# Moving the four blocks of a small second product from the first two column tiles to the seventh, in a fused decoder layer on one Trainium2 core

## Chip, core and metric

The kernel runs on one core of one Trainium2 chip. A core has TensorE (PE: products, and with a separate row the weight loads PEld), VectorE (DVE), ScalarE (ACT), GpSimd (POOL) and SyncE (SP); the last two here issue DMAs for the most part. The metric is the device time of one execution in microseconds, lower is better; the time of before is the median of three runs.

## The reference

One layer, 512 tokens, width 2048. Cut to what matters:

```python
h = rms_norm(x, norm_gain)
z = h @ w_in                                   # 2048 x 6656
q, k, v, g_attn, c_b, c_c, c_h, g_conv = split(z)
q, k = partial_rope(rms_norm(q)), partial_rope(rms_norm(k))   # heads of 64
y_attn = sliding_window_attention(q, k, v, sinks) * silu(g_attn)   # 16 heads, 4 KV heads, window 128
y_conv = c_b * short_conv(c_c * c_h, conv_w) * silu(g_conv)
x = x + concat([y_attn, y_conv]) @ w_out
gate = sigmoid(rms_norm(x, gate_gain) @ w_ple_gate + b)
e = rms_norm(p @ w_ple_proj, ple_norm_gain)    # p: 512 x 256, w_ple_proj: 256 x 2048
out = x + gate * e
```

`e` is needed only by the last two of the kernel's groups; attention's output is needed by its sixth.

## The kernel before

Everything is fp32, as products of split halves (`wh`, `wl`: ScalarE casts the high half, line 199, VectorE subtracts for the low one, line 200), three matmuls for each product. The kernel has three stages. The first computes K and V and one group of Q's columns. The last computes eight groups by a scheme with seven products in place of eight (line 241). Between them lies the stage that is changed: lines 711 to 905, about 126 to 274 us of the profiled execution.

In this stage a loop computes the first half of c_c and c_h, in column tiles of 128 columns by 512 tokens: `gemm_tile` runs 16 steps `k` of three matmuls each (48 in all, PSUM tile `psg`), and the tiles alternate c_c and c_h. Seven tiles are computed in the loop; the eighth is computed after it (line 1391, PSUM `pst`). Each tile has two weight loads ("jobs") of 512 KB, `raw`. `next_job` splits one job ahead and fetches two more.

After every second `k`, thus every six matmuls, `tick()` advances a clock and runs what was registered for it with `at(when, ...)`, in order of time and then of registration. TensorE's order is just the order in which the Python code emits it; the order on the other four engines in this stage is decided by a scheduler. Registered are:

- `make_k(t)`, ticks 4 and 7: transposes K into PSUM `psm` (one buffer), which ScalarE evicts into `kr` (line 740); then four casts `khh` and four differences `kll`.
- `square_q`, `rstd_q`, `rope_q`: head norm and rotation of the half of Q that is used last.
- `attention(j, n, when)`, 16 units (KV head j, block n), each of four pieces. `scores` (line 794, PSUM `pss`, room for one unit; then VectorE's four reductions, line 800, into `prob`, of which there are two; then ScalarE's exponentials, line 807); `turn` (transposes of `prob` into `pst`, line 822, and halves `pth`, `ptl`); `values` (line 832, PSUM `pso`, copied to `up` and stored by a DMA); and an accumulating DMA. For even n, `turn_q` four ticks earlier transposes Q into the same `psm` and copies it to two tiles `st` (lines 776, 777).
- `e_block(n)`, through a table `mids` that names the tile and the `k` ahead of which it is emitted: 24 matmuls into four PSUM banks (both tiles of `pss`, and two of `pst`). Each bank is then squared with a row sum by ScalarE (line 865), multiplied by the gain `pg` by VectorE (line 867) and stored to memory by a DMA on POOL's queue (line 868).

`up`, `kr`, `yconv`, `pg` and e's tiles share one pool of eleven buffers. At the end of the stage its memory goes to the weight tiles of the last stage (`wy`, `ws`), whose loads wait until the DMAs that read the old tiles have landed.

Of the kernel before, what the change touches and what calls it, by code (L numbers as in the profile page):

```python
# [27 lines left out]
TQ, TK, TV, TGA, TCB, TCC, TCH, TGC = 0, 8, 10, 12, 20, 28, 36, 44  # L28
# [7 lines left out]
def hymba_layer(ctx: ExitStack, tc: tile.TileContext, io):  # L36
# [87 lines left out]
    for g in range(NG):  # L124
        w, n = groups[g]
# [72 lines left out]
    def halves(h, l, src):  # L198
        nc.scalar.copy(h, src)  # L199
        tt(l, src, f32(h), op=ALU.subtract)  # L200
# [259 lines left out]
    def flat(t):  # L460
        return t.rearrange("p a b -> p (a b)")
# [32 lines left out]
    for c in range(8):  # L494
# [20 lines left out]
        for i in range(2):  # L515
            k = 2 * c + i
# [47 lines left out]
    def head_sums(z, out, junk):  # L564

        sq = junk.rearrange("p (h d) -> p h d", d=HD)
        nc.scalar.activation(sq, z, AF.Square)
        nc.vector.tensor_reduce(out, sq, axis=mybir.AxisListType.X, op=ALU.add)

    def head_rstd(ms, eps):  # L570


        stt(ms, ms, 1.0 / HD, eps.unsqueeze(2).broadcast_to(ms.shape), op0=ALU.mult, op1=ALU.add)
        power(ms, ms)
# [8 lines left out]
    def q_of(t, n):  # L583
        return qs[t, n].rearrange("p b (h d) -> p b h d", d=HD)
# [3 lines left out]
    def square_q(t, n, b, junk):  # L588
        if b == 0:
            rq[t, n] = small.tile([P, 2, 8], F32, name="msq", bufs=4)  # L590
        head_sums(q_of(t, n)[:, b], rq[t, n][:, b], junk("sqq"))

    def rstd_q(t, n):
        blocks = slice(2 * t, 2 * t + 2)
        head_rstd(rq[t, n], eps_tok[:, blocks])

    def rope_q(t, n):
        rope(q_of(t, n), 0, slice(2 * t, 2 * t + 2), mtile)
# [5 lines left out]
    for j, s in enumerate((6, 6, 7, 7, 9, 9, 10, 10)):  # L604
        soon(after, s, form7, j)

    jobs = [io["w_in"][TCC, 0], io["w_ple_proj"][0], io["w_in"][TCC, 1], io["w_ple_proj"][1],
            io["w_in"][TCH, 0], io["w_ple_proj"][2], io["w_ple_proj"][3], io["w_in"][TCH, 1]]
    for i in range(1, 4):
        jobs += [io["w_in"][t + i, c] for t in (TCC, TCH) for c in range(2)]  # L610
    raws, splits, job = {}, {}, [0]

    def blocks_of(t):
# [68 lines left out]
    def mtile(name):  # L682
        return misc.tile([P, T], F32, tag="m", name=name)
# [5 lines left out]
    def at(when, fn):  # L689
        later.append((when, len(later), fn))  # L690
# [31 lines left out]
    for t in range(2):  # L722
        rope_q(t, 1)
        for b in range(2):
            at(18 + 2 * t + b, lambda t=t, b=b: square_q(t, 0, b, mtile))
        at(20 + 2 * t, lambda t=t: rstd_q(t, 0))
        at(24 + 2 * t, lambda t=t: rope_q(t, 0))
    mask = cw.tile([P, 2 * P], F32, name="mask", bufs=1)
    nc.gpsimd.dma_start(mask, io["mask"])
    vv = vvp.tile([P, NB, NKV, 2, HD], F32R, name="vv")  # L730
# [51 lines left out]
    def attention(j, n, when):  # L782

        lo = 0 if n else P
        cell = {}

        def scores():
            sc = [ps_s.tile([P, 2, 2 * P], F32, name="pss") for _ in range(2)]
            ks = slice(n * P + lo - P, (n + 1) * P)
            for r in range(4):  # L790
                i = 2 * (n % 2) + r // 2
                q = turned[j, n // 2, r % 2][:, i * P : (i + 1) * P]
                out = sc[r // 2][:, r % 2, lo:]
                nc.tensor.matmul(out, q, khh[j][:, ks], start=True, stop=False)
                nc.tensor.matmul(out, q, kll[j][:, ks], start=False, stop=True)
            t = ap.tile([P, 4, 2 * P], F32, name="prob")
            negm, sums, sk = (small.tile([P, 4], F32, name=x) for x in ("negm", "sums", "sk"))
            r_q = rq[n // 2, j // 2][:, n % 2, 4 * (j % 2) : 4 * (j % 2) + 4]
            for r in range(4):
                nc.vector.tensor_tensor_reduce(  # L800
                    t[:, r, lo:], sc[r // 2][:, r % 2, lo:], mask[:, lo:], HD**-0.5, NEG,
                    ALU.add, ALU.max, negm[:, r : r + 1],
                )
            tt(negm, negm, r_q, op=ALU.mult)
            stt(negm, negm, -1.0, nsink[:, 4 * j : 4 * j + 4], op0=ALU.mult, op1=ALU.min)
            for r in range(4):
                nc.scalar.activation(  # L807
                    t[:, r, lo:], t[:, r, lo:], AF.Exp, scale=r_q[:, r : r + 1], bias=negm[:, r : r + 1],
                    accum_out=sums[:, r : r + 1],
                )  # L810
            tt(sk, sink[:, 4 * j : 4 * j + 4], negm, op=ALU.add)
            nc.scalar.activation(sk, sk, AF.Exp)
            tt(sums, sums, sk, op=ALU.add)
            nc.vector.reciprocal(rs[:, n, 4 * j : 4 * j + 4], sums)
            cell["t"] = t

        def turn():
            cell["pt"] = []
            for kt in range(lo // P, 2):
                pt_ = ps_t.tile([P, T], F32, name="pst")  # L820
                for r in range(4):
                    nc.tensor.transpose(pt_[:, r * P : (r + 1) * P], cell["t"][:, r, kt * P : (kt + 1) * P], ident)  # L822
                h, l = (ap.tile([P, T], F32R, name=x) for x in ("pth", "ptl"))
                halves(h, l, pt_)
                cell["pt"].append((n - 1 + kt, h, l))

        def values():
            po = ps_o.tile([P, 4, P], F32, name="pso")
            pts = cell["pt"]
            for i, (b, h, l) in enumerate(pts):  # L830
                w = vv[:, b, j].rearrange("p s d -> p (s d)")
                nc.tensor.matmul(po, w, h, start=i == 0, stop=False)  # L832
                nc.tensor.matmul(po, w, l, start=False, stop=i == len(pts) - 1)
            up = mtile("up").rearrange("p (r t) -> p r t", t=P)
            nc.scalar.copy(up, po)
            rows = attn_dram[j].rearrange("(r d) (n t) -> d r n t", d=HD, n=NB)[:, :, n]
            nc.gpsimd.dma_start(rows, up[:HD])
            cell["add"] = lambda: nc.gpsimd.dma_start(rows, up[HD:], accum_op=ALU.add)

        if n % 2 == 0:  # L840
            at(when - 4, lambda: turn_q(j, n // 2))
        at(when, scores)
        at(when + 5, turn)
        at(when + 8, values)
        at(when + 12, lambda: cell["add"]())

# [3 lines left out]
    def load_pg(n):  # L850
        pgs.append(mtile("pg"))
        nc.sync.dma_start(pgs[n], io["ple_norm_gain"][:, n * T : (n + 1) * T])

    def e_block(n):

        pg = pgs[n]
        if n < 3:
            load_pg(n + 1)
        ws = next_job()
        banks = [flat(ps_s.tile([P, 2, 2 * P], F32, name="pss")) for _ in range(2)]  # L860
        banks += [ps_t.tile([P, T], F32, name="pst") for _ in range(2)]

        def take_e(t):
            e = mtile("e")
            nc.scalar.activation(e, banks[t], AF.Square, accum_out=esq[:, t, n : n + 1])
            e = mtile("e")
            tt(e, banks[t], pg, op=ALU.mult)
            nc.gpsimd.dma_start(e_dram[t // 2][n][:, t % 2], e)

        for t in range(NB):  # L870
            for k in range(2):
                h, l = (a[:, k, t * P : (t + 1) * P] for a in pts)
                for i, (a, w) in enumerate(((h, ws[0]), (l, ws[0]), (h, ws[1]))):
                    nc.tensor.matmul(banks[t], a, w[:, k], start=k == 0 and i == 0, stop=k == 1 and i == 2)  # L874
            for i in (t,):
                take_e(i)
# [1 line left out]
    load_pg(0)  # L878
    order = [(j, n) for j in (2, 3, 0, 1) for n in range(NB)]
    for u, (j, n) in enumerate(order):  # L880
        attention(j, n, 13 + 35 * u // 15)
    mids = {0: {8: lambda: e_block(0)}, 1: {k: lambda n=n: e_block(n) for n, k in ((1, 0), (2, 4), (3, 8))}}


    for i in range(4):
        ps = gemm_tile(ps_g.tile([P, T], F32, name="psg"), mids.get(2 * i))
        zc = mtile("zc") if i < 3 else rowp.tile([P, T], F32, tag="rows", name="zc")
        tt(zc, ps, rx2, op=ALU.mult)
        if i == 3:
            break  # L890
        ps = gemm_tile(ps_g.tile([P, T], F32, name="psg"), mids.get(2 * i + 1))
        u = cw.tile([P, T + HD], F32, name="u")
        nc.gpsimd.memset(u[:, 0:2], 0.0)
        tt(u[:, 2 : T + 2], ps, zc, op=ALU.mult)
        y = mtile("yconv")
        nc.scalar.activation(y, u[:, 0:T], AF.Copy, scale=convw[:, 0, i : i + 1])
        for s in (1, 2):
            stt(y, u[:, s : s + T], convw[:, s, i : i + 1], y, op0=ALU.mult, op1=ALU.add)
        nc.gpsimd.dma_start(conv_dram[i], y)
# [493 lines left out]
    u, y = itile("u"), rowp.tile([P, T], F32, tag="rows", name="yconv")  # L1393
# [121 lines left out]
```

## Time and profile before

| | |
|---|---|
| median of three runs | 919.99 us (919.91 to 920.25) |
| profiled execution | 919.36 us |
| its span, first to last instruction | 917.6 us |
| granted TensorE clock | 0.998 |
| TensorE busy | 905.9 us, 99% of the span |
| VectorE, ScalarE, GpSimd busy | 723.8, 542.7, 160.8 us |
| DMA | 195.06 MB, mean 213 GB/s |
| this stage begins, and its eighth tile begins | 126.34 us, 274.28 us |

Times in the profile are counted from the span's start. A busy TensorE is modelled from pipelined matmuls: starts are what counts, not durations. A row of the wait list reads: who waited, for whom, microseconds in total, how often, the longest.

### The profile page before, as it was taken

The numbers are of one execution on the slowest core, as the hardware profiler recorded it, in microseconds if no ns is written. First come the engines' busy times: TensorE is split into PE (matmuls) and PEld (weight loads), VectorE is DVE, ScalarE is ACT, GpSimd is POOL, SyncE is SP. The second block draws the span as 40 slices with busy tenths as digits, with TensorE's granted clock in tenths as the row PEclk, the third lists the DMA queues.
The fourth block names the chain that finished last, engine by engine and source line by source line (L and its number), as shares of the span: only waits on it lengthen the run. The fifth ranks groups of instructions, "written<-read, shape, count | busy, mean of one in ns | idle before, by whom it ended". The sixth has DMA issues, their size and how long they took to land.

```text
span 917.6 us, 12067 instructions
## 1 busy us (share of the span) xinstructions
PE 905.9 (99%) x4178; PEld 751.4 (82%) x4178; DVE 723.8 (79%) x1063; ACT 542.7 (59%) x878; POOL 160.8 (18%) x211
## 2 busy tenths in 40 slices
PE   9999999999999999999999999999999999999997
PEld 8888888878888888888888888888888888887885
DVE  6878888788765777877768678987858887889678
ACT  6767847778863443454345357766556666555453
POOL 4232132143230001100120110102120111001100
PEclk9999999999999999999999999999999999999999
DMA  9999558434469767558578887858996993588647
GB/s 315 362 292 308 197 63 309 162 81 108 93 116 313 269 204 234 159 169 233 157 185 240 239 222 233 253 141 229 341 291 193 211 295 92 139 248 267 183 138 218
DMA packets 71389, 195.06 MB, mean 213 GB/s; under 512 B 8355, under 2 KB 14819, under 8 KB 71328
## 3 DMA queue, kind: packets, MB, share of 16 engines
q1 hardware_dynamic: 48096, 132.14, 42.3%
q0 software_dynamic: 23088, 62.15, 30.5%
q8 instruction: 32, 0.52, 0.2%
q14 instruction: 29, 0.24, 0.1%
q10 hardware_dynamic: 144, 0.01, 0.0%
HBM read 162.81 MB, written 31.46 MB: 212 GB/s over the span
## 4 chain that ended last, share of the span: by engine, by line
PE 89%; DVE 6%; ACT 3%; issue 2%; DVEq 0%; ACTq 0%
PE psp L241 67%; PE psg L711 6%; PE psp L519 5%; PE pst L241 4%; PE pst L993 2%; ACT prob L807 1%; PE pss L874 1%; PE pst L1391 1%; PE pst L874 1%; PE pst L822 1%; DVE wl L200 1%; DVE z L1289 1%; DVE prob L800 1%; DVE ptl L200 1%; PE pso L832 1%
## 5 line engine op out<-in xcount | busy, mean ns | idle before, releaser
L241 PE MATMUL psp<-wh,form 128*128 128x512 f32 x1280 | 395.3, 390 | 0.0
L241 PEld LDWEIGHTS psp<-wh,form 128*128 128x128 f32 x1280 | 239.4, 188 | 49.2
L241 PE MATMUL psp<-wl,form 128*128 128x512 f32 x640 | 249.5, 390 | 1.3 <-DVE wl L200 1.2
L200 DVE TENSOR_TENSOR wl<-wy,wh 128x1024 fp32r<-128x1024 f32 x108 | 131.5, 1222 | 60.3 <-ACT wh L199 59.7
L199 ACT CAST wh<-wy 128x1024 fp32r<-128x1024 f32 x108 | 113.4, 1051 | 90.2 <-PE psp L241 70.6
L241 PEld LDWEIGHTS psp<-wl,form 128*128 128x128 f32 x640 | 120.1, 188 | 27.4 <-DVE wl L200 2.5
L200 DVE TENSOR_TENSOR wl<-wx,wh 128x1024 fp32r<-128x1024 f32 x72 | 88.0, 1223 | 50.0 <-ACT wh L199 49.8
L199 ACT CAST wh<-ws 128x1024 fp32r<-128x1024 f32 x72 | 75.9, 1054 | 74.5 <-PE psp L241 53.8
L199 ACT CAST wh<-wx 128x1024 fp32r<-128x1024 f32 x72 | 75.6, 1052 | 74.3 <-PE psp L241 52.7
L241 PE MATMUL psp<-wh,hsh 128*128 128x512 f32 x304 | 118.6, 390 | 0.0
L241 PE MATMUL psp<-wl,hsh 128*128 128x512 f32 x304 | 118.3, 389 | 0.0
L241 PE MATMUL psp<-wh,hsl 128*128 128x512 f32 x304 | 118.3, 389 | 0.0
L200 DVE TENSOR_TENSOR wl<-ws,wh 128x1024 fp32r<-128x1024 f32 x72 | 88.1, 1223 | 27.1 <-ACT wh L199 26.8
L189 DVE TENSOR_TENSOR wy<-wy,ws 128x1024 f32<-128x1024 f32 x72 | 87.7, 1218 | 0.0
L241 PEld LDWEIGHTS psp<-wh,hsh 128*128 128x128 f32 x304 | 57.1, 188 | 11.8
L241 PEld LDWEIGHTS psp<-wh,hsl 128*128 128x128 f32 x304 | 57.1, 188 | 11.8
L241 PEld LDWEIGHTS psp<-wl,hsh 128*128 128x128 f32 x304 | 57.1, 188 | 11.8
L711 PE MATMUL psg<-hsh,wh 128*128 128x512 f32 x112 | 45.2, 403 | 0.0
L711 PE MATMUL psg<-hsh,wl 128*128 128x512 f32 x112 | 43.8, 391 | 0.0
L711 PE MATMUL psg<-hsl,wh 128*128 128x512 f32 x112 | 43.8, 391 | 0.0
L199 ACT CAST wh<-raw 128x1024 fp32r<-128x1024 f32 (+1 forms) x29 | 29.2, 1006 | 22.5 <-DMA raw<-in_w_ple_proj 7.7
L200 DVE TENSOR_TENSOR wl<-raw,wh 128x1024 fp32r<-128x1024 f32 (+1 forms) x29 | 33.8, 1165 | 9.5 <-ACT wh L199 9.2
(218 smaller groups left out, 1307.1 us busy)
## 6 DMA issues: line engine op xcount, KB each, us to landing
ws<-in_w_mid SPq DMA_DIRECT2D x40, 512.0 KB, 4.5
wx<-in_w_mid SPq DMA_DIRECT2D x24, 512.0 KB, 4.2
wy<-in_w_mid SPq DMA_DIRECT2D x20, 512.0 KB, 7.6
h<-form POOLq DMA_DIRECT2D x32, 256.0 KB, 5.8
wy<-in_w_mid POOLq DMA_DIRECT2D x16, 512.0 KB, 8.1
raw<-in_w_in SPq DMA_DIRECT2D x16, 512.0 KB, 4.1
wx<-in_w_out SPq DMA_DIRECT2D x16, 512.0 KB, 7.6
ws<-in_w_out SPq DMA_DIRECT2D x16, 512.0 KB, 5.6
```

The lines of the kernel that those rows point to most:

```text
L189: tt(y, y, got[g, "s1" if f == 6 else "s0", c], op=ALU.add)
L199: nc.scalar.copy(h, src)
L200: tt(l, src, f32(h), op=ALU.subtract)
L241: nc.tensor.matmul(ps[t], a, w[:, i], start=start and first and i == 0 and n == 0, stop=last and i == 1 and n == 2, skip_group_check=not s ...
L519: nc.tensor.matmul(kv_ps[t // 2][:, t % 2], hs[k][a][:, t * P : (t + 1) * P], kv_split[c][w][:, i], start=k == 0 and n == 0, stop=k == KT ...
L711: nc.tensor.matmul(ps, w[:, k % 8], a, start=k == 0 and n == 0, stop=k == KT - 1 and n == 2)
L800: nc.vector.tensor_tensor_reduce(t[:, r, lo:], sc[r // 2][:, r % 2, lo:], mask[:, lo:], HD**-0.5, NEG, ALU.add, ALU.max, negm[:, r : r + 1],)
L807: nc.scalar.activation(t[:, r, lo:], t[:, r, lo:], AF.Exp, scale=r_q[:, r : r + 1], bias=negm[:, r : r + 1], accum_out=sums[:, r : r + 1],)
L822: nc.tensor.transpose(pt_[:, r * P : (r + 1) * P], cell["t"][:, r, kt * P : (kt + 1) * P], ident)
L832: nc.tensor.matmul(po, w, h, start=i == 0, stop=False)
L874: nc.tensor.matmul(banks[t], a, w[:, k], start=k == 0 and i == 0, stop=k == 1 and i == 2)
L993: nc.tensor.transpose(pt[:, b], quads[b // 2][:, b % 2, f * P : (f + 1) * P], ident)
```

## The change

Five edits in one stage, no change of what is computed.

- `mids`: e's blocks 0 to 2 move from tiles 0 and 1 to tile 6, ahead of its steps 8, 10 and 12; block 3 follows after that tile.
- `jobs`: the four loads of `w_ple_proj` stand accordingly at places 13, 15, 16 and 17 of 20 instead of 1, 3, 5 and 6.
- attention's units are registered two ticks earlier (first scores at tick 11 instead of 13); Q's turns, the values and the accumulating DMA move along with them, by two.
- `turn` comes six ticks after its unit's scores instead of five, thus in all one tick earlier than before.
- squares, norm and rotation of Q's other half come three ticks earlier.

```diff
-    jobs = [io["w_in"][TCC, 0], io["w_ple_proj"][0], io["w_in"][TCC, 1], io["w_ple_proj"][1],
-            io["w_in"][TCH, 0], io["w_ple_proj"][2], io["w_ple_proj"][3], io["w_in"][TCH, 1]]
-    for i in range(1, 4):
-        jobs += [io["w_in"][t + i, c] for t in (TCC, TCH) for c in range(2)]
+    jobs = [io["w_in"][t + i, c] for i in range(4) for t in (TCC, TCH) for c in range(2)]
+    jobs[13:14] = [io["w_ple_proj"][0], jobs[13]] + [io["w_ple_proj"][i] for i in range(1, 4)]
...
-            at(18 + 2 * t + b, lambda t=t, b=b: square_q(t, 0, b, mtile))
-        at(20 + 2 * t, lambda t=t: rstd_q(t, 0))
-        at(24 + 2 * t, lambda t=t: rope_q(t, 0))
+            at(15 + 2 * t + b, lambda t=t, b=b: square_q(t, 0, b, mtile))
+        at(17 + 2 * t, lambda t=t: rstd_q(t, 0))
+        at(21 + 2 * t, lambda t=t: rope_q(t, 0))
...
-        at(when + 5, turn)
+        at(when + 6, turn)
         at(when + 8, values)
...
-        attention(j, n, 13 + 35 * u // 15)
-    mids = {0: {8: lambda: e_block(0)}, 1: {k: lambda n=n: e_block(n) for n, k in ((1, 0), (2, 4), (3, 8))}}
+        attention(j, n, 11 + 35 * u // 15)
+    mids = {6: {k: lambda n=n: e_block(n) for n, k in ((0, 8), (1, 10), (2, 12))}}
...
         if i == 3:
+            e_block(3)
             break
```

Below is what stands in a row on the engines at three places. A row is the line, the operation, the tiles written and read, and the size; line numbers after the change are smaller by two.

TensorE around K's second transposes (`psm<-ident,kv`), before and then after the change; `psm<-ident,z` are Q's transposes.

```order
L711 MATMUL psg<-hsl,wh 128x512
L711 MATMUL psg<-hsh,wl 128x512
L739 MATMUL psm<-ident,kv 128x128 x4
L711 MATMUL psg<-hsh,wh 128x512
L711 MATMUL psg<-hsl,wh 128x512
```

```order
L709 MATMUL psg<-hsl,wh 128x512
L709 MATMUL psg<-hsh,wl 128x512
L737 MATMUL psm<-ident,kv 128x128 x4
L770 MATMUL psm<-ident,z 128x128 x4
L709 MATMUL psg<-hsh,wh 128x512
```

Both sets of transposes now follow each other into the one buffer `psm`; and 18 products of c_c stand between the first transposes of K and these, where there were 18 products and an e block.

ScalarE at the same place, before and then after: `wh<-raw` is a weight cast, `kr` evicts `psm`.

```order
L199 CAST wh<-raw 128x1024
L740 ACTIVATE kr<-psm,kq 128x512
L745 CAST khh<-kr 64x512
L746 CAST khh<-kr 64x512
L745 CAST khh<-kr 64x512
L746 CAST khh<-kr 64x512
L865 ACTIVATE e,esq<-pss 128x512 x2
L865 ACTIVATE e,esq<-pst 128x512
L199 CAST wh<-raw 128x1024
L865 ACTIVATE e,esq<-pst 128x512
L740 ACTIVATE kr<-psm,kq 128x512
```

```order
L199 CAST wh<-raw 128x1024
L738 ACTIVATE kr<-psm,kq 128x512
L743 CAST khh<-kr 64x512
L744 CAST khh<-kr 64x512
L743 CAST khh<-kr 64x512
L744 CAST khh<-kr 64x512
L738 ACTIVATE kr<-psm,kq 128x512
L743 CAST khh<-kr 64x512
```

The first eviction keeps its place behind the weight cast; e's four squares and a cast have gone from between the two evictions.

TensorE in attention, at the fourth unit's scores (`pss_2005` before, `pss_1756` after), with buffer numbers; `prob_1863` is the second unit's `prob`, `prob_1572` the first's.

```order
L711 MATMUL psg_1895<-hsl_373,wh_1792 128x512
L711 MATMUL psg_1895<-hsh_372,wl_1793 128x512
L822 MATMUL pst_1987<-ident_208,prob_1863 128x128 x4
L822 MATMUL pst_1996<-ident_208,prob_1863 128x128 x4
L794 MATMUL pss_2005<-khh_1455,st_1835 128x256
```

```order
L820 MATMUL pst_1738<-ident_208,prob_1572 128x128 x4
L709 MATMUL psg_1719<-hsh_252,wh_1609 128x512
L709 MATMUL psg_1719<-hsl_253,wh_1609 128x512
L709 MATMUL psg_1719<-hsh_252,wl_1610 128x512
L709 MATMUL psg_1719<-hsh_258,wh_1609 128x512
L709 MATMUL psg_1719<-hsl_259,wh_1609 128x512
L709 MATMUL psg_1719<-hsh_258,wl_1610 128x512
L792 MATMUL pss_1756<-khh_1455,st_1595 128x256
```

Before, the second unit is already turned when the fourth unit's scores come; after, only the first is, and the second follows the scores.

## The prediction

> **What bounds the kernel now.** I read the page first: engines and chain.
>
> ```profile
> span 917.6 us, 12067 instructions
> PE 905.9 (99%) x4178; PEld 751.4 (82%) x4178; DVE 723.8 (79%) x1063; ACT 542.7 (59%) x878; POOL 160.8 (18%) x211
> PE 89%; DVE 6%; ACT 3%; issue 2%; DVEq 0%; ACTq 0%
> ```
>
> TensorE carries 89% of the chain, so a microsecond counts only if TensorE waits for it. Next the windows over the stage that is changed (about 126 to 274 us), with the columns stretch, length, busy time of PE, PEld, DVE, ACT, POOL, granted clock, DMA share, GB/s.
>
> ```profile
> 126.00:134.00 8.00, 8.00 (x39) 6.63 (x38) 7.08 (x24) 1.98 (x2) 0.00 (x0) 1.00 0.53 26
> 134.00:166.00 32.00, 32.00 (x147) 26.49 (x146) 24.58 (x33) 22.96 (x49) 7.63 (x14) 1.00 0.88 303
> 166.00:246.00 80.00, 77.06 (x445) 65.49 (x444) 65.81 (x238) 65.05 (x176) 24.84 (x27) 1.00 0.43 101
> 246.00:286.00 40.00, 39.81 (x197) 33.16 (x197) 20.40 (x55) 21.77 (x49) 11.92 (x15) 1.00 0.67 159
> ```
>
> In attention's stretch (166 to 246) VectorE and ScalarE are each busy 82% (65.8 and 65.1 of 80) and TensorE loses 2.9 us. In the stretch of e's blocks (134 to 166) TensorE loses nothing. Third, TensorE's waits in this stage (total, times, longest) and the chain in order of time.
>
> ```profile
> PE pst L822 <- DVE ptl L200: 2.4, 3, 1.5
> PE pst L822 <- DVE negm L804: 0.6, 1, 0.6
> PE pso L832 <- ACT up L835: 0.2, 1, 0.2
> ```
>
> ```profile
> 126.34 5.45 PE psg L711 x24
> 131.78 0.44 PE psm L739 x4
> 132.22 2.75 PE pss L874 x12
> 134.98 2.72 PE pst L874 x12
> 137.70 4.08 PE psg L711 x18
> 141.78 0.44 PE psm L739 x4
> ...
> 274.28 10.88 PE pst L1391 x48
> ```
>
> One e block is 2.75 + 2.72 = 5.47 us of products, a tick (six products) 1.36. The stage lasts 274.28 - 126.34 = 147.9 us. Before, 5.5 us of e stand between the first transposes of K (131.78) and the next (141.78).
>
> **The change, part by part.** Four e blocks leave the front and return at the end: 4 x 5.47 us of TensorE work moves, none goes. What matters is what they covered.
>
> *The front.* K's second transposes (make_k(0)) stay at tick 7, but without the block TensorE gets there at 126.34 + 5.45 + 0.44 + 4.08 = 136.3 instead of 141.78. Attention's first turn of Q moves from tick 9 to the same tick 7, directly behind. All three use the single PSUM buffer psm, which is free only when ScalarE has evicted it (L740, kr). ScalarE's rows there:
>
> ```profile
> 135.80 1.05 ACT L199 CAST wh<-raw 128x1024 fp32r<-128x1024 f32 x1 [7.67 <-DMA raw<-in_w_ple_proj]
> 136.75 0.68 ACT L740 ACTIVATE kr<-psm,kq 128x512 f32<-128x512 f32 x1
> ...
> 139.40 0.62 ACT L746 CAST khh<-kr 64x512 fp32r<-64x512 f32 x1
> ```
>
> ScalarE stood 7.67 us for a weight load, and the first kr is queued behind that cast. In the new order the same cast (now of a w_in tile, the fourth load, of the same size, behind the same instructions) stands ahead of kr, so kr again ends at 136.75 + 0.68 = 137.4. TensorE waits 137.5 - 136.3 = 1.2 us. The transposes take 0.44. The new order has the second kr behind four casts khh, the last of which ends at 139.40 + 0.62 = 140.0; kr ends at 140.7, and Q's transposes start then: 140.75 - 137.95 = 2.8 us more. Together 4.0 us. Bounds: 0 if the load landed 4 us sooner; 7.67 is all that ScalarE stood, so up to 7 if it came that much later. I take 4.0, since everything ahead of the load is unchanged.
>
> *The first scores*, now at tick 11, 24 products later: 141.2 + 5.45 = 146.65. They need Q's two halves st, behind the second kr (140.7), four khh, st, one weight cast and two more ScalarE casts, then VectorE's weight difference and st itself. With 0.62, 0.59, 1.05, 1.23 and 0.69 from the rows here and below that ends at 147.2: 0.5 us (bounds 0 to 1.5). Before, e's blocks covered this chain for 22 us.
>
> *The loop.* A unit's scores fill pss (room for one unit); VectorE's four reductions (L800) empty it into prob (two buffers), ScalarE exponentiates, TensorE turns prob into pst, halves follow, then values. The reduction of unit u writes prob's buffer of unit u-2, so it waits for the turn of u-2.
>
> ```profile
> L800 DVE CUSTOM_DVE_ANT_0 prob<-pss,mask 128x256 f32<-128x256 f32 x48 | 17.9, 420 | 2.6 <-PE pst L822 2.4 <-PE pss L795 0.2
> ```
>
> Before, VectorE idled 2.4 us on that. Before, units whose scores are 5 ticks apart from those of u-2 find the turn done; now the turn comes at 6, after scores of u in every unit and exactly one tick ahead of scores u+1 (the spacing is 7 ticks per three units). So the ring is: turn of u-2, reduction of u on VectorE, scores of u+1 on TensorE, with six products (1.36 us) of cover where there were two ticks. Rows of a unit:
>
> ```profile
> 219.69 1.03 PE L822 MATMUL pst<-ident,prob 128*128 128x128 f32 x8
> 223.64 0.42 DVE L800 CUSTOM_DVE_ANT_0 prob<-pss,mask 128x256 f32<-128x256 f32 x1
> 223.99 0.42 DVE L800 CUSTOM_DVE_ANT_0 prob<-pss,mask 128x256 f32<-128x256 f32 x1
> 224.53 1.29 DVE L200 TENSOR_TENSOR ptl<-pst,pth 128x512 fp32r<-128x512 f32 x2
> 226.09 0.59 ACT L807 ACTIVATE prob<-prob,negm,msq 128x256 f32<-128x256 f32 x1
> 226.22 1.23 DVE L200 TENSOR_TENSOR wl<-raw,wh 128x1024 fp32r<-128x1024 f32 x1
> 217.59 0.59 ACT L776 CAST st<-psm 64x512 fp32r<-64x512 f32 x1
> 219.74 0.69 DVE L777 TENSOR_TENSOR st<-psm,st 64x512 fp32r<-64x512 f32 x1
> ```
>
> Reductions start 0.35 us apart: two free half of pss after 0.8 us, four take 1.4 to 1.5. A free VectorE just fits under 1.36 us; one that is late stalls TensorE by as much. It runs late where a weight difference (1.23) or the sums, which wait for four exponentials (4 x 0.59), stand ahead of the reduction. I walked the new order of the three engines by hand with these durations. Eight places are late, by 0.9, 0.6, 1.3, 1.1, 0.4, 0.3, 0.2 and 0.5 us: 5.3 us, an estimate from these rows. Bounds: 0 (VectorE always free) and 14 us (fourteen reductions late by 1 us each). I take the walk. It holds the squares and rotations of Q too, which come three ticks earlier, one beside the scores. TensorE's waits of before (L822, above) leave, since turns come after scores that have waited already.
>
> *What was lost before.* The walk ends the stage after 153.2 us, 10.1 of them waits (4.0 + 0.5 + 5.3 + 0.3, the last from the next part), so 143.1 are work. Before, 147.9 - 143.1 = 4.8 us were lost: 3.2 named in the waits above, 1.6 in restarts.
>
> *The end.* e's blocks stand between the last turns and values, where VectorE and ScalarE have room (20.4 and 21.8 of 40 us).
>
> ```profile
> L865 ACT ACTIVATE e<-pss x8: 582/594/600, 139.9 to 163.2; 128x512 f32<-128x512 f32 x8
> L867 DVE TENSOR_TENSOR e<-pss,pg x8: 681/688/693, 140.9 to 163.9; 128x512 f32<-128x512 f32 x8
> 274.13 2.23 SPq L158 DMA_DIRECT2D wy<-in_w_mid  x4
> 276.45 10.40 SPq L158 DMA_DIRECT2D ws<-in_w_mid  x3
> 286.94 4.10 SPq L1415 DMA_DIRECT2D form<-h  x8
> 282.06 1.02 POOL L838 DMA_DIRECT2D a<-up  x1 [6.21 <-DMA a<-up]
> ```
>
> A bank is emptied by 0.59 and 0.69 one after the other, within the next bank's 1.36 us. Only the last conv tile waits: it takes the third bank of block 3, emptied 0.3 us late (bounds 0 to 1). Sixteen stores of e now go through POOL's queue at the end, and the loads wy and ws into the memory they leave wait for them: I expect the last store's landing 8 us into the last conv tile. Before, the same SP queue already stood for attention's last add (issued at 282.06) and let forms go at 286.94, 12.7 us into that tile, and no TensorE wait followed. So 0, with a bound of 4 if forms come that much later. On SP's queue four pg loads and four weight loads move behind attention's; the stretch's DMA share is 0.67, so I cost them at 0, covered by that room.
>
> *Sum:* 10.1 - 4.8 = +5.3 us. The profiled execution took 919.36 us (span 917.6), the median of the runs is 919.99, 0.6 more; so 924.7 in a profile, 925.3 for the median.
>
> **The rivals.** 1. *The loop falls behind* (slower still): every unit's reduction is about 1 us late, 14 us in place of 5.3: 934. For it: 82% on two engines that wait for each other. Against: the walk finds many units in time. Chance 0.12.
>
> 2. *The fourth load lands sooner* (the other side). It took the longest of the loads around the stage's start, while loads from w_in, which it now is, land in 4.1 us at the median:
>
> ```profile
> raw<-in_w_in SPq DMA_DIRECT2D x16, 512.0 KB, 4.1
> DMA to landing us min/median/max: 7.6/10.0/13.7
> ```
>
> If the 13.7 us came with the old data, the cast is done before K's first transposes. Then kr follows those at once, the four khh end before 136.3, and the front loses some 0.6 us (one kr) in place of 4.0; the first scores lose nothing, and VectorE enters the loop 4 us ahead, which covers its first three late places (2.8 us). 0.6 + 2.5 + 0.3 - 4.8 = -1.4: 918.6. It decides where the loop loses under 2.1 us: then it is faster by over 0.2%. Against: the load has the same size, issue and neighbours as before, and all loads near it were slow (least 7.6). Chance 0.12, half of it faster.
>
> 3. *The loop loses little:* the front costs its 4.8 us in all, which only swaps with the 4.8 of before: 920.0, and up to 921.8 (0.2%, about what a measurement of this kernel can tell from no change) if the loop loses up to 1.8. For it: no turn waits in the new order. Against: engines 82% busy. Chance 0.11.
>
> 4. *The clock.* The granted clock is 1.00 even where TensorE is busy only 2.55 of 4 us:
>
> ```profile
> 186.00:190.00 4.00, 2.55 (x20) 2.23 (x20) 3.89 (x12) 3.41 (x11) 4.00 (x3) 1.00 0.02 4
> ```
>
> The front's wait, 2.8 us in one piece, is longer than any wait there (1.5). If the clock halved behind it, the 24 products up to the first scores would take up to 5.45 us more: 931. Chance 0.05. The Trainium skill, page "TensorE: Matmul & The Clock Gate", section "Part 1: The HAM clock gate", says that an idle window of about 3.4 us halves the clock; by that rule, which no wait here tests, the 2.8 us would not do it, but 4.0 us broken by one short burst might.
>
> **How the numbers follow.** My forecast (front lost, loop partly: 922 to 929) has 0.60, rival 1 0.12, rival 2 0.12, rival 3 0.11, rival 4 0.05. Range: 920 to 931, which leaves out rival 1's 0.12 and what of rival 2 lies below 920, some 0.08. Slower: 0.60 + 0.12 + 0.05 = 0.77; same: 0.11 + 0.06 = 0.17; faster: 0.06.
>
> **What would show it.** In the profile after: TensorE waiting at psm for ScalarE's kr, twice, near 136 and 138 us, 4 us in all; no waits at the turns; waits of the scores (pss) for the reductions, and VectorE's reductions idle on the turn; the last conv tile starting near 279.5; from there the same durations as before. I am wrong if the fourth weight load lands early, if the loop's waits exceed 8 us or vanish, or if wy, ws or forms come late enough to open gaps after the last conv tile.

## The result, and the profile after

The changed kernel takes 925.09 us (median of four runs, 924.75 to 925.30), the kernel before beside it 919.95 (919.68 to 920.25): 1.0057 times as long, 95% interval 1.0045 to 1.0070, thus slower by 5.1 us. The profiled execution took 924.75 us. Head of its page, busy times and chain:

```profile
span 923.0 us, 12050 instructions
PE 909.0 (98%) x4178; PEld 751.5 (81%) x4178; DVE 723.8 (78%) x1063; ACT 544.0 (59%) x878; POOL 160.7 (17%) x211
PE 69%; DVE 2%; issue 1%; ACT 1%; DMA 0%; DVEq 0%; ACTq 0%
```

The span grew by 5.4 us and the amount of work did not: VectorE is busy for the same 723.8 us. The same windows as before, with two short ones where the front's wait ends (columns as in the prediction):

```profile
126.00:134.00 8.00, 8.00 (x39) 6.62 (x38) 7.40 (x25) 1.98 (x2) 0.00 (x0) 1.00 0.59 58
134.00:166.00 32.00, 28.11 (x140) 22.68 (x140) 25.01 (x65) 23.83 (x51) 3.61 (x3) 0.95 0.36 126
140.00:142.00 2.00, 1.89 (x8) 1.60 (x9) 1.48 (x3) 1.92 (x4) 0.00 (x0) 0.68 0.84 344
142.00:144.00 2.00, 2.00 (x6) 1.52 (x6) 1.94 (x4) 1.97 (x3) 0.00 (x0) 0.50 0.08 29
166.00:246.00 80.00, 78.28 (x442) 65.71 (x440) 61.37 (x226) 63.03 (x173) 24.65 (x28) 1.00 0.47 98
```

From 134 to 166 us TensorE now loses 3.9 us where it lost nothing, and the granted clock falls to 0.50 in the middle of it. TensorE's waits in the stage, from 120 to 292 us:

```profile
PE psm L770 <- ACT kr L738: 2.6, 1, 2.6
PE pss L792 <- DVE negm L798: 1.7, 3, 0.7
PE pso L831 <- DVE ptl L200: 1.3, 2, 0.7
PE psm L737 <- ACT kr L738: 0.6, 1, 0.6
PE pst L1390 <- DVE e L865: 0.2, 1, 0.2
```

The turns (before: `pst`, line 822, 3.0 us) wait no more; `psm`, `pss` and `pso` wait instead. The front, ScalarE's rows and then TensorE's, from the timeline:

```profile
135.13 1.05 ACT L199 CAST wh<-raw 128x1024 fp32r<-128x1024 f32 x1 [7.09 <-DMA raw<-in_w_in]
136.09 0.68 ACT L738 ACTIVATE kr<-psm,kq 128x512 f32<-128x512 f32 x1
139.37 0.69 ACT L738 ACTIVATE kr<-psm,kq 128x512 f32<-128x512 f32 x1
...
136.82 0.66 PE L737 MATMUL psm<-ident,kv 128*128 128x128 f32 x4 [0.57 <-ACT kr L738]
140.11 0.66 PE L770 MATMUL psm<-ident,z 128*128 128x128 f32 x4 [2.63 <-ACT kr L738]
140.52 0.62 PE L709 MATMUL psg<-hsh,wh 128*128 128x512 f32 x1
140.94 0.63 PE L709 MATMUL psg<-hsl,wh 128*128 128x512 f32 x1
```

The double wait stands where it was forecast: the cast waits for the load, `kr` stands behind the cast, and the second `kr` behind four `khh`. Behind the wait, products start 0.42 us apart instead of 0.23, for eight products. VectorE's reductions now idle 6.7 us, 6.5 of it on a turn (before, as the prediction shows, 2.6 and 2.4), and the turns themselves wait for nothing; by groups (busy, mean ns | idle before them):

```profile
L798 DVE CUSTOM_DVE_ANT_0 prob<-pss,mask 128x256 f32<-128x256 f32 (+1 forms) x60 | 20.7, 390 | 6.7 <-PE pst L820 6.5
L820 PE MATMUL pst<-ident,prob 128*128 128x128 f32 x112 | 14.8, 272 | 0.0
```

The end: the eighth tile in the chain; the SP queue behind it; and the first product of the last stage, before and after.

```profile
281.29 11.18 PE pst L1390 x48
284.75 3.09 SPq L158 DMA_DIRECT2D wy<-in_w_mid  x4
289.89 9.00 SPq L1414 DMA_DIRECT2D form<-h  x8
...
285.00 0.39 PE L241 MATMUL psp<-wh,hsh 128*128 128x512 f32 x1
292.30 0.39 PE L241 MATMUL psp<-wh,hsh 128*128 128x512 f32 x1
```

The eighth tile starts 7.0 us later than before (274.28), the last stage 7.3 us. Yet the span is only 5.4 us longer, so 1.9 us come back later. Where, one wait of the kernel before shows, together with ScalarE's and GpSimd's rows ahead of it (the last two are of the changed kernel):

```profile
PE psp L241 <- DVE wl L200: 1.2, 1, 1.2
807.72 0.86 POOL L1266 DMA_DIRECT2D z<-in_b_ple_gate  x1 [25.16 <-DVE wl L200]
816.24 1.06 ACT L1285 ACTIVATE z<-z 128x1024 f32<-128x1024 f32 x1 [2.33 <-DMA z<-in_b_ple_gate]
...
814.07 0.86 POOL L1265 DMA_DIRECT2D z<-in_b_ple_gate  x1 [24.13 <-PE psp L241]
821.30 1.06 ACT L1284 ACTIVATE z<-z 128x1024 f32<-128x1024 f32 x1
```

Before, ScalarE's sigmoid near 816 us waits 2.33 us for the bias that a DMA adds; the weight cast queued behind it is late, VectorE's difference `wl` with it, and TensorE waits 1.2 us near 827. After, the DMA is issued 0.95 us sooner when counted from the last stage's start (814.07 - 292.30 against 807.72 - 285.00), the sigmoid does not wait, and no wait of TensorE is listed in the last stage. By the products' starts TensorE loses 1.9 us between 815 and 840 us before and 0.1 after, which is the whole of what comes back.

For the comparisons below I summed TensorE's losses from its timeline: between two successive products, the distance of their starts less the usual distance for such a pair of shapes (one or two ns of scatter in each of some 2800 products add up to the 4 us that the last column has in every kernel). Front: the first 22 us of the stage. Loop: from there to 300 us, the eighth tile included. Rest: behind it. Each ratio is to the kernel before as it ran beside that kernel on the same chip (medians 919.70 to 919.98 us).

| | time, us | ratio to before (95%) | front | loop | rest |
|---|---|---|---|---|---|
| before | 919.95 | | 0.3 | 7.8 | 6.1 |
| changed | 925.09 | 1.0057 (1.0045 to 1.0070) | 5.3 | 10.0 | 4.3 |
| changed, second time | 923.93 | 1.0045 (1.0032 to 1.0057) | 4.7 | 9.9 | 4.2 |
| K behind Q's turn | 923.96 | 1.0044 (1.0030 to 1.0058) | 4.4 | 10.4 | 4.2 |
| filled wait | 923.50 | 1.0041 (1.0028 to 1.0053) | 1.2 + 2.5 of filling | 10.9 | 4.2 |
| turn at five | 922.04 | 1.0027 (1.0018 to 1.0037) | 4.4 | 8.1 | 4.2 |
| early store | 922.22 | 1.0026 (1.0016 to 1.0035) | 1.9 | 10.6 | 4.2 |
| early store, turn at five | 920.36 | 1.0008 (0.9999 to 1.0017) | 1.9 | 8.6 | 4.3 |
| before, turn at six | 919.88 | 0.9999 (0.9990 to 1.0008) | 0.3 | 8.1 | 6.5 |
| before, early store | 919.36 | 0.9996 (0.9987 to 1.0005) | 0.3 | 8.3 | 6.3 |
| e alone | 919.16 | 0.9989 (0.9980 to 0.9998) | 1.3 | 8.3 | 4.2 |
| e alone, early store | 917.92 | 0.9977 (0.9968 to 0.9986) | 0.5 | 7.9 | 4.2 |
| the same, two memsets more | 917.63 | 0.9977 (0.9967 to 0.9987) | 0.5 | 7.7 | 4.2 |
| before, two memsets on VectorE | 919.70 | 0.9998 (0.9990 to 1.0007) | 0.3 | 7.7 | 6.1 |

The change by this table: front +5.0, loop +2.2, rest -1.8.

### The profile page after: what moved, and what is told of

It reads as the page before. It is cut to its first block, busy times and chain, and to the rows that moved or that the text cites. A ratio compares the mean times of both kernels' runs of the same rounds, so it can differ in the third digit from the quotient of the medians.

```text
span 923.0 us, 12050 instructions
## 1 busy us (share of the span) xinstructions
PE 909.0 (98%) x4178; PEld 751.5 (81%) x4178; DVE 723.8 (78%) x1063; ACT 544.0 (59%) x878; POOL 160.7 (17%) x211
## 4 chain that ended last, share of the span: by engine, by line
PE 69%; DVE 2%; issue 1%; ACT 1%; DMA 0%; DVEq 0%; ACTq 0%
PE psp L241 59%; PE pst L241 4%; PE pst L992 2%; PE pst L1390 1%; PE pss L872 1%; PE pst L872 1%; PE psg L709 1%; DVE z L1288 1%; DVE wl L200 0%; DMA wx<-in_w_out 0%; DVE wy L189 0%; ACT z L1111 0%; DVE form L200 0%; ACT z L998 0%; PE pso L831 0%
## 5 line engine op out<-in xcount | busy, mean ns | idle before, releaser
L805 ACT ACTIVATE prob<-prob,negm,msq 128x256 f32<-128x256 f32 (+1 forms) x64 | 36.0, 565 | 15.7 <-DVE negm L803 15.6
```

Source lines behind the costliest of these rows:

```text
L805: nc.scalar.activation(t[:, r, lo:], t[:, r, lo:], AF.Exp, scale=r_q[:, r : r + 1], bias=negm[:, r : r + 1], accum_out=sums[:, r : r + 1],)
```

## The experiments

**K behind Q's turn.** Does the loss go if the two transposes no longer follow each other into `psm`?

```diff
-    at(7, lambda: make_k(0))
+    at(9, lambda: make_k(0))
...
-            st = rowp.tile([P, T], F32R, tag="rows", name="st")
+            if (j, t) == (2, 0):
+                st = misc.tile([P, T], F32R, tag="m", name="st")
+            else:
+                st = rowp.tile([P, T], F32R, tag="rows", name="st")
```

> K's second transposes go from tick 7 to tick 9, behind attention's first turn of Q, so that the two sets no longer follow each other into the one buffer psm (the first two st take buffers of the pool misc, since K and V still hold those of rows). Theory A (the front's double wait and the half clock behind it are real losses): of the waits at psm only some 0.6 us stays, the clock stays at 1.00 from 140 to 144 us, no wait at the first scores; the last conv tile starts 4 us sooner, at 277, and the time is about 920.5 to 921.5. Rival B (VectorE and ScalarE pace the loop, so what TensorE gains at its front it waits for later): the waits at the scores grow by as much, 924 to 925.

923.96 us. A wait at `psm` and a window in the middle of what followed:

```profile
PE psm L737 <- DVE st L778: 2.2, 1, 2.2
142.00:144.00 2.00, 2.00 (x7) 1.56 (x6) 1.21 (x3) 1.98 (x4) 0.00 (x0) 0.62 0.29 90
```

Neither theory held. The wait changed places: now K's transposes wait, for VectorE, whose difference `st` still reads `psm`; the clock halves again. One buffer that two engines read one after the other makes whoever comes second wait. The edit did not remove the loss, so it says nothing on what the loss is worth.

**Filled wait.**

```diff
     at(7, lambda: make_k(0))
+    def fill():
+        d = ps_t.tile([P, T], F32, name="pst")
+        for i in range(11):
+            nc.tensor.matmul(d, pts[0][:, 0, :P], pts[0][:, 0], start=i == 0, stop=i == 10)
+    at(7, fill)
```

> Eleven products that nobody reads stand between K's second transposes and Q's turn, so TensorE works where it waited 2.6 us. Leaves nothing out, adds 11 x 0.227 = 2.5 us of work. Theory A (the clock halves because of the idle time): granted clock 1.00 from 140 to 144 us, the 8 products at 0.425 us apart come at 0.227, 1.6 us less; but the first scores then come at 146.1 and wait for st, which VectorE ended at 146.8, so 0.75 us of it is lost again: net 0.8 to 1.6 us faster than the changed kernel, 923.5 to 924.3. Rival C (the half clock is not due to the idle time): the clock drops as before, time unchanged or longer, 925 to 927.

923.50 us, at the lower end of what theory A gave. The window and the first scores:

```profile
140.00:142.00 2.00, 2.00 (x10) 1.66 (x9) 1.96 (x4) 1.94 (x5) 0.00 (x0) 1.00 0.19 74
PE pss L799 <- DVE st L782: 0.5, 1, 0.5
```

With TensorE at work the clock stays at 1.00: the idle time had halved it. And the first scores now wait 0.5 us for `st`, the term that the prediction had and the changed kernel did not show: the half clock had covered it. The front loses 3.7 us in all (2.5 of it the filling) against 4.7 in the changed kernel's second run, and the loop loses 1.0 more (10.9 against 9.9). So the half clock costs 1.6 us at its place, most of which is lost again behind it when it is gone. What it is worth in the whole, 0.4 to 1.5 us by the ratios (1.0041 against the changed kernel's 1.0045 and 1.0057, whose intervals overlap with it), is not settled.

**Turn at five**, in the changed kernel.

```diff
-        at(when + 6, turn)
+        at(when + 5, turn)
```

> The turn of a unit comes five ticks after its scores again, all else as in the changed kernel. Theory A (the sixth tick trades waits of the turns for waits of the scores): waits of the scores (1.7 us, three times) shrink below 1, waits of the turns on the exponentials return with 2 to 3 us; 0 to +1.5 us against the changed kernel, 925 to 926.5. Rival D (the sixth tick is what makes the loop lose): scores' waits go and nothing comes back, 923.5 or less.

922.04 us, below either run of the changed kernel (the intervals of the ratios, 1.0018 to 1.0037 and 1.0032 to 1.0057, still touch for its second run). Its waits:

```profile
PE psm L770 <- ACT kr L738: 2.4, 1, 2.4
PE pst L820 <- DVE ptl L200: 1.1, 2, 0.6
PE pst L820 <- DVE negm L802: 1.0, 2, 0.7
PE pso L830 <- ACT up L833: 0.5, 2, 0.3
```

The waits did trade places as theory A had it (2.1 us of turns for 1.7 of scores and most of 1.3 of values), but the time is rival D's. The difference lies in losses under 0.2 us apiece, no row of the wait list: in the loop 4.0 us of them here, 5.8 in the changed kernel, spread over products of all kinds. What stops each of them was not traced, so the sixth tick is shown to cost the changed kernel some 2 us, and how it does so is not.

**Before, turn at six.** The same edit, the other way round, in the kernel before.

> The kernel before with one edit, the turn six ticks after its scores instead of five. Theory A (the sixth tick costs the loop some 2 us by itself, through waits of the scores and a restart after each): loop loses 10 us in place of 7.9, waits named at the scores, none at the turns: 921.5 to 922. Rival F (the sixth tick hurts only where the units come two ticks earlier, with VectorE behind from the front): 919.5 to 920.2.

```profile
PE pss L794 <- DVE negm L800: 1.8, 2, 1.1
PE psp L241 <- DVE wl L200: 1.3, 2, 1.2
```

919.88 us: no change, rival F. The small losses rise here too (from 3.9 to 5.4 us), but the named ones fall (from 3.9 to 2.7): the ring of reduction and scores stalls at two places only. The sixth tick costs some 2 us in the changed kernel and nothing in the kernel before. Three things differ between the two, the units' two ticks, e's place and the three ticks of Q's squares; which of them makes the sixth tick dear was not separated.

**Early store.** Why is the fourth load late?

```diff
-    soon(after, 23, lambda: nc.gpsimd.dma_start(r_dram.rearrange("b p -> p b"), rx2_tok))
+    soon(after, 22, lambda: nc.gpsimd.dma_start(r_dram.rearrange("b p -> p b"), rx2_tok))
```

> The store of rows_r (512 writes of four bytes on GpSimd's queue) is issued ahead of GpSimd's norm of Q instead of behind it, some 3 to 5 us sooner. Theory A (the fourth weight load lands late because those writes hold up the DMA engines): the load lands by 131 us instead of 135.1, ScalarE's cast and the first kr follow K's first transposes at once, the front's waits at psm fall from 3.2 to 0.7 us and the clock stays at 1.00; about 4 us faster than the changed kernel, 920 to 921.5. Rival E (the load is late for another reason, the loads ahead of it on the queue): it lands at 134 to 135.5 as before, 924.5 to 925.5.

922.22 us. GpSimd's issue, ScalarE's cast, the wait that stays (the last row: the changed kernel's issue):

```profile
116.10 0.81 POOL L647 DMA_DIRECT2D rows_r<-rx_tok  x1
131.87 1.05 ACT L199 CAST wh<-raw 128x1024 fp32r<-128x1024 f32 x1 [3.46 <-PE psg L709]
PE psm L770 <- ACT kr L738: 0.8, 1, 0.8
...
120.72 0.81 POOL L647 DMA_DIRECT2D rows_r<-rx_tok  x1
```

With the store issued 4.6 us sooner the cast waits for the loop's products, no longer for the load, the waits at `psm` are down to 0.8 us and the clock stays whole. The cause of the front is thus shown to the end of its chain: the scattered store holds up the fourth load. By which way (the engines' time, or order on a queue) is not shown. The gain is smaller than expected (920 to 921.5) since the loop takes 0.7 us back and the first scores wait 0.4.

**The changed kernel a second time**, beside the next three.

> The changed kernel itself once more, beside the next three on one chip, since in three kernels that change nothing ahead of it the fourth load landed 1 us sooner than in the changed kernel's profile. Expected 924 to 925.2 us by theory A: if the load lands 1 us sooner the front waits 1 us less.

923.93 us, just under what was expected. ScalarE's cast started at 134.36 us:

```profile
134.36 1.05 ACT L199 CAST wh<-raw 128x1024 fp32r<-128x1024 f32 x1 [6.37 <-DMA raw<-in_w_in]
```

So the load's landing differs between runs by 0.8 us, and the front's first wait of 0.6 us with it; the second stays at 2.6.

**e alone.** The moved blocks and loads of the change, with `when` from 13, the turn at five and the squares as before.

```diff
-        attention(j, n, 11 + 35 * u // 15)
+        attention(j, n, 13 + 35 * u // 15)
...
-        at(when + 6, turn)
+        at(when + 5, turn)
```

> e's blocks and their loads moved as in the changed kernel, nothing else: units at 13, turn at five ticks, squares and rotation as before. Theory A: Q's first turn comes two ticks (2.7 us of products) behind K's second transposes, so the wait there is under 0.7 us and the clock stays at 1.00; the loop loses what it lost before (7.9 us); if the stall of 1.8 us near 823 us is gone as in all kernels so far with e's blocks in the seventh tile, 918.5 to 919.5, else 920 to 921. Rival G (e's blocks at the end cost by themselves, or the uncovered front costs in any order): 922 or more.

919.16 us: faster than the kernel before by a hair (interval 0.9980 to 0.9998). Its waits in the whole rest of the program:

```profile
PE pst L820 <- DVE ptl L200: 2.3, 3, 1.5
PE pss L792 <- DVE st L775: 0.6, 1, 0.6
PE pst L820 <- DVE negm L802: 0.5, 1, 0.5
PE pso L830 <- ACT up L833: 0.2, 1, 0.2
```

No wait at `psm`, no half clock, the turns' waits as before, none in the last stage. The same uncovered front with the same late load costs 1.0 us more than before when Q's turn stands two ticks behind K's transposes. So the move of e's blocks is not what made the change slow. The front's loss comes with the units' two ticks, which put Q's turn directly behind K's, and the loop's with the sixth tick. The three ticks of Q's squares went along with the units' in every kernel and were not timed by themselves; they start at tick 15, behind the front's waits.

**e alone, early store**, both edits.

> As the one before, with the store of rows_r issued ahead of GpSimd's norm of Q. Theory A: the fourth load lands 3 us sooner, so the last of the front's waits goes too: 0 to 1 us faster than without, 918 to 919. Rival H (attention paces itself after that, the cover is not needed): the same as without.

917.92 us, 0.23% under the kernel before (interval 0.9968 to 0.9986) and faster than both kernels of this study. The front loses 0.5 us.

**Before, early store.**

> The kernel before with one edit: the store of rows_r issued ahead of GpSimd's norm of Q. Theory A (before, e's first block covered the late load): the load lands 3 us sooner, but TensorE waits no less, 919.5 to 920.2. Rival K (the load's lateness cost the kernel before something too, through the loop): 918.5 or less, as much as the same edit brought where e's blocks stand at the end (1.2 us).

919.36 us, no change: the cast starts at 130.95 us instead of 135.80, and TensorE had not waited for it. (The profiled execution has a half clock of its own in attention, at 188.78 us; see the end.) The same edit that is worth 1.2 us where the front is bare is worth nothing under e's first block.

**Early store, turn at five**, in the changed kernel.

> The changed kernel with the store issued early and the turn at five ticks: the units are still two ticks earlier. Theory A (front and turn add up): the front loses 1.9 us as with the store alone, the loop 8.1 as with the turn alone: 919.8 to 920.8. Rival L (one of the two edits already took what the other takes): 921.5 to 922.3.

920.36 us: the two edits add up, as theory A had it. What is left of the excess over before (ratio 1.0008, interval 0.9999 to 1.0017) can't be told from nothing.

**The stall near 827 us.** Two kernels shift GpSimd's instruction by two places, one each way.

```diff
         nc.gpsimd.memset(u[:, 0:2], 0.0)
+        if i < 2:
+            nc.gpsimd.memset(u[:, 0:2], 0.0)
```

```diff
-        nc.gpsimd.memset(u[:, 0:2], 0.0)
+        (nc.vector if i < 2 else nc.gpsimd).memset(u[:, 0:2], 0.0)
```

> The fastest kernel so far (e's blocks moved alone, early store) with two more memsets of two columns on GpSimd in the changed stage, twice the same zeros. In the kernel before GpSimd's third bias add of the first gate group is issued 2.95 us after VectorE's join began, in all kernels with e's blocks in the seventh tile after 1.93; ScalarE's sigmoid then waits 2.3 us, and TensorE 1.3 near 827 us. Theory I (where in GpSimd's program that issue stands decides it, two places later here): the stall comes back, 919.2 to 920. Rival J (e's blocks or the state of the queues decide it): 917.6 to 918.4.

> The kernel before with two of its three memsets of two columns on VectorE in place of GpSimd. Theory I: the bias add stands two places earlier in GpSimd's program, its issue comes 1.93 us after the join, TensorE's stall near 827 us is gone, 918 to 918.5. Rival J (the place in the program does not matter): the stall stays, 919.7 to 920.1.

917.63 (ratio 0.9977, 0.9967 to 0.9987) and 919.70 us (0.9998, 0.9990 to 1.0007). GpSimd's rows, of the first and of the second:

```profile
806.57 0.86 POOL L1267 DMA_DIRECT2D z<-in_b_ple_gate  x1 [24.12 <-PE psp L241]
...
807.53 0.86 POOL L1266 DMA_DIRECT2D z<-in_b_ple_gate  x1 [25.15 <-DVE wl L200]
```

Theory I falls: the stall kept away in the one and stayed in the other. In all four kernels with e's blocks at the front GpSimd's issue comes one microsecond later after VectorE's join than in all nine with the blocks in the seventh tile, though order and dependencies there are the same. So far as these thirteen kernels go e's place decides it, with the loads and stores that go along; how, stays open.

## Why the prediction came out right, point by point

The time, 925.1 against 925.3, the place of the loss and its order of size were right; of the terms several were off, and they cancelled: front +5.0 where the sum had +4.5, loop and end +2.2 where it had +0.8, the rest of the program -1.8 where it had nothing. That the number came within 0.2 us is luck; the double wait at `psm` is not.

- *The front.* Both waits at `psm` stand near 136 and 138 us for the reason given, 3.2 us of waits in place of 4.0: the load landed 0.7 us sooner (its cast started at 135.13 instead of 135.80), which took half of the first wait of 1.2. The second was 2.6 of 2.8.
- *The clock*, rival 4, was given 0.05 as a way of its own that ends at 931. It came about, as an addition: eight products at half pace, 1.6 us, not 24 products and 5.45. The step that failed is the pricing: a halving was taken to last up to the first scores; the records show 3.41 us. Part of the 1.6 us was cover for the next item. The Trainium skill's page "TensorE: Matmul & The Clock Gate", section "Part 1: The HAM clock gate (the "warmup" mystery)", gives a window of that length, 3413 ns, and the trace agrees. Its condition of an idle window is not what the traces show, see the end.
- *The first scores*, 0.5 us: 0 in the changed kernel, covered by the half clock; 0.5 as soon as the clock was kept up.
- *The loop*, 5.3 us of late places less the 4.8 us lost before. Named waits came to 3.0 us, at five places and not eight, two of them at the values (`pso`, 1.3), which the walk did not have: in the changed kernel they follow the turn by two ticks instead of three, and with the turn at five this wait on `ptl` is gone. But the sum also counted the 1.6 us of restarts before as gone, and the losses under 0.2 us apiece, where restarts would show, grew from 3.9 to 5.8 us. By starts the loop lost 10.0 us against 7.8. That is the mis-sized term: +2.2, the end's 0.2 in it, where the sum had +0.8 (5.3 + 0.3 - 4.8). The losses of 0.2 us and more hardly grew (3.9 to 4.2), so the ring makes the scores wait as forecast (1.7 us), mostly in place of the turns' waits, and the growth lies in small losses whose cause is open. So the eighth tile began at 281.29, not 279.5.
- *The end*: 0.2 us of 0.3; `wy`, `ws` and forms came without any wait. `form` was let go 8.6 us into the eighth tile (289.89 - 281.29).
- *What came after the stage* was put at no change. It gave 1.8 us back, a stall in the last stage that only kernels with e's blocks at the front have. This step was missing, and without it the time would have been near 927.
- *Rivals 1 to 3.* The loop did not fall behind: 3.0 us of named waits, not 14. The fourth load landing at the early end would have given 922.2 with the change as it is (early store), not 918.6: the loop's loss stays. Rival 3's condition, a loop that loses no more than before, holds for these units only without the sixth tick.
- *A reading.* ScalarE's 65.05 us of 80 are 81%, not 82; nothing hangs on it.

## What to carry to other kernels

Work between two uses of a single PSUM buffer is cover, so its move is priced at that buffer: who reads it last, on which queue, behind what. Time each edit of a bundle by itself: here the blocks' move alone gained 0.1%, and the shifts bundled with it cost 0.6 to 0.7%. Count losses by the products' starts and not by named waits alone, over the whole program, since a stall far behind the change can go or come with it.

## What the hardware showed beyond expectation

The clock. A short wait halves TensorE's granted clock for 3.41 us. Five profiles have one such record ahead of the program's end: the changed kernel twice, K behind Q's turn, turn at five, and before, early store. Stretches of 3.41 us just before and during it, of the changed kernel and of K behind Q's turn; then the one just before it in before, early store; and last one of the kernel before, which no half clock followed:

```profile
137.30:140.71 3.41, 0.78 (x7) 0.60 (x6) 2.89 (x5) 3.28 (x6) 0.00 (x0) 1.00 0.99 379
140.71:144.13 3.42, 3.42 (x10) 2.65 (x9) 3.31 (x5) 3.33 (x7) 0.00 (x0) 0.50 0.33 133
...
139.06:142.48 3.42, 1.24 (x8) 1.15 (x9) 3.20 (x4) 1.69 (x3) 0.00 (x0) 1.00 0.39 157
142.48:145.89 3.41, 3.41 (x10) 2.66 (x9) 2.71 (x5) 3.34 (x7) 0.00 (x0) 0.50 0.42 154
...
185.37:188.78 3.41, 1.95 (x17) 1.71 (x17) 3.33 (x7) 2.83 (x9) 3.41 (x3) 1.00 0.02 5
...
184.20:187.61 3.41, 1.96 (x10) 1.33 (x8) 3.18 (x15) 3.35 (x9) 3.41 (x2) 1.00 0.00 0
```

TensorE was busy for 0.78, 1.24 and 1.95 us of the 3.41 before the halving, and in before, early store a wait of 1.5 us in one piece was enough. So a whole idle window, as that page of the Trainium skill has it, was not needed here.

The windows can be placed in every profile: the changed kernel's half clock at 140.70 us and the one behind its last product, at 922.36, are 229.0 times 3.413 us apart, and the records of all fourteen profiles fit such a grid. Busy time does not tell which window halves the clock: 1.95 us did and 1.96 did not, nor did 1.51 at the end of the changed kernel (915.53 to 918.94). The work started in the window does, as far as these profiles go: counted in columns, 128 for a transpose and 512 for a product of the loop, the nineteen windows with a half clock behind them (fourteen of them at the program's end) have at most 2560, the 3719 others, from the first full clock on, at least 2560. The window at 185.37 us had sixteen starts of 128, the one at 184.20 seven of 512 and one of 128. Products 0.227 us apart would start some 7700 columns in a window, so the limit here is about a third of that, an estimate from these counts.

The store. A scattered store of 2 KB issued at 120.72 us goes with a 512 KB load that lands at 135.0; issued 4.6 us sooner, with one that lands at 129.4. In all fourteen profiles the fourth load lands 3.6 to 4.1 us after the store has landed, as long as a load of `w_in` takes at the median (4.1). From issue to landing it takes 12.1 to 13.7 us in the nine profiles with the store as it was and 7.0 to 7.3 in the five with the early store, so even the early store may still delay it.
